# Moving the split weights' tiles by 64 bytes within the on-chip memory, in a two-block transformer kernel

## The chip, the cores and the metric

The kernel runs on one core of a Trainium2 chip. The metric is the device time of one execution, in microseconds (us). Before the change it is 1656.22 us, the median of three runs (1655.35 to 1659.63). Lower is better.

## The reference

Two small networks follow each other, all in float32, on 256 positions of width 1024. The first block has two layers. In each, a conditioning vector is multiplied with `w_ada` and gives shifts, scales and gates; a normed and modulated input is multiplied with `w_in`; a pooling mixer and a differential attention over 512 keys follow, then `w_out`, and a squared-relu MLP of width 4096. The first layer does this for the positions `x` and for the context `ctx`, the second for `x` alone. The second block has one layer with block attention and gated linear attention and one with a gated recurrence, each with a convolutional feed-forward network of width 3072.

```python
for l in range(DEPTH):                       # first block
    h = modulate(rms_norm(x, g_mix[l]), sa, ca)
    u, q, k, v = split_heads(h @ w_in[l])
    ...
    x = x + ga * (mix @ w_out[l])
    x = x + gm * sq_relu_mlp(modulate(rms_norm(x, g_mlp[l]), sm, cm), w_mlp1[l], w_mlp2[l])
for l in range(DEPTH):                       # second block
    h = h + mix
    h = h + conv_ffn(rms_norm_2(h, ffn_norm_g[l]), ffn_w_up[l], ffn_conv_w[l], ffn_conv_b[l], ffn_w_down[l])
```

What matters here: nearly all of the work is products of a [1024 or more, n] weight matrix, read once from HBM, with 256 (or 2 x 256) positions.

## The kernel before, in words

**The split products.** TensorE takes operands of type float32r here, which keep fewer bits than float32. To stay exact enough, each operand is held as two parts: `hi`, its value cast to float32r, and `lo`, the cast of what is left. A product is three matmuls: hi x hi, hi x lo and lo x hi. `unit` (L582) makes the list of calls and `issue` (L591) issues them, all on L593. Each is a matmul of a stationary 128x128 piece of the weights (`whi` or `wlo`) and a moving 128x256 piece of the data (`hid`, `fhi`, `flo`, `h2hi`, `dhi` and so on). There are 11,232 of them in the program, each with its own weight load.

**The stream of weights.** `Stream` (L72 to L175) brings every weight matrix in pieces of 1 MB: a DMA on SP fills a tile `raw` (three buffers of 8192 bytes in each partition). Each piece is two units of 128x1024 numbers. For a unit ScalarE casts `raw` to `whi` (L111), and VectorE subtracts and writes `wlo` (L119); there are four buffers of 4096 bytes of each. A unit feeds 24 matmuls on L593: 16 with `whi` (hi and lo data), then 8 with `wlo`, in the order of four output tiles. The order of all work is written out in the program: `gemm` (L597) issues six or so matmuls, steps a late eviction, lets the stream make a step (`tick`) and goes on.

**The conditioning.** Columns of `w_ada` come as tiles `araw` of 4096 bytes; VectorE multiplies them with a scalar column of `cs` and adds up (L278, L280), or TensorE does it with `cs` stationary (L293, L840) or `cr`, the split of `cs` (L837).

**Where the tiles lie.** Four pools stand one behind the other in each partition of the on-chip memory: `wp` (`raw`, `whi`, `wlo`, `araw`), `sp` (all data tiles and scratch), `cp` (constants and the residual `X`) and `mp` (small tiles). Within a pool, tags lie in the order of their first use. In `sp` the four buffers of `hid` follow each other in steps of 8192 bytes, and the six buffers of the other operands (`hhi`, `h2hi`, `fhi`, `dhi` ... with their lo parts) in steps of 8320. A `hid` or `fhi` piece k begins 1024 k bytes into its buffer; the pieces of `dhi` and `dlo`, where they carry two columns more (258), begin 1032 k bytes into it.

The lines that the change touches are L29 (which tags are small), L183 to L195 (the pools and `scr`), L755 and L823 (`cs` and `cr`).

Of the kernel before, what the change touches and what calls it, by code (L numbers as in the profile page):

```python
# [8 lines left out]
F32 = mybir.dt.float32  # L9
F32R = mybir.dt.float32r  # L10
# [15 lines left out]


MARKS = None
SMALL = {"tiny", "tiny4", "gs", "ared", "asum", "acol", "ld", "m2", "z2", "edge", "rtok", "gng", "aq4"}  # L29


def shape_constants():
# [141 lines left out]
def body(tc, I, out, dbg=None, stop=None):  # L174
    from contextlib import ExitStack  # L175
    with ExitStack() as es:
        _body(es, tc, I, out, dbg, stop)


def _body(es, tc, I, out, dbg, stop):  # L180
    nc = tc.nc
    mm, act, dve, pool_e, pe = nc.tensor.matmul, nc.scalar, nc.vector, nc.gpsimd, nc.tensor

    wp = es.enter_context(tc.tile_pool(name="wp", bufs=2))
    sp = es.enter_context(tc.tile_pool(name="sp", bufs=2))
    cp = es.enter_context(tc.tile_pool(name="cp", bufs=1))
    mp = es.enter_context(tc.tile_pool(name="mp", bufs=2))
    ps = es.enter_context(tc.tile_pool(name="ps", bufs=8, space=PSUM))
    st = Stream(nc, wp)

    def bank(shape=(128, 2, T)):
        return ps.tile(list(shape), F32, tag="ps", bufs=8, name="ps")

    def scr(shape, tag="s", bufs=5, dt=F32):
        return (mp if tag in SMALL else sp).tile(list(shape), dt, tag=tag, bufs=bufs, name=tag)  # L195

    def scr1(shape=(128, T)):
        return scr(shape, tag="s1", bufs=6)
# [17 lines left out]
    def mark(name):  # L216
        if MARKS is not None:
            MARKS.append((name, nc.next_id()))
# [47 lines left out]
    def ada_part(l, j, nv, ch, q):  # L266
# [20 lines left out]
        def rows(raw):  # L287

            if q == 0:
                acc[1] = bank([128, 512])  # L290
            p = acc[1]
            for k in range(2):
                mm(p[:2], cs[:, :, 2 * q + k], raw[:, k], start=q == 0 and k == 0, stop=q == 3 and k == 1)  # L293
            if q == 3:
                r = sp.tile([2, 512], F32, tag="aacc", bufs=1, name="arow")
                act.copy(r, p[:2])
                yield False
                c0 = 8 * j + 4 * ch
                p = bank([128, 8])
                for i in range(4):  # L300
                    pe.transpose(p[:, 2 * i:2 * i + 2], r[:, 128 * i:128 * i + 128], ident[:2, :2])
                yield False
                dve.tensor_add(ada[l][:, :nv, c0:c0 + 4], p[:, :8].rearrange("p (i v) -> p v i", v=2)[:, :nv],
                               pcol("b_ada", 48 * l + c0, 4)[:, None].to_broadcast([128, nv, 4]))
                if ch == 1:
                    done.add((l, j))
            yield True
# [3 lines left out]
    def ada_reduce(l, j, nv, ch, a):  # L311
        red = scr([128, 2, 16], tag="ared", bufs=1)
        for v in range(nv):
            dve.transpose(a[:, v], a[:, v])
            dve.reduce_sum(red[:, v], a[:, v].rearrange("p (b q) -> p b q", q=32), axis=AX)
        q4 = scr([32, 3, 2, 16], tag="aq4", bufs=1)
        for g in range(3):
            pool_e.tensor_copy(q4[:, g, :nv], red[32 * g + 32:32 * g + 64, :nv])
        s = scr([32, 2, 16], tag="asum", bufs=1)
        pool_e.tensor_add(q4[:, 0, :nv], q4[:, 0, :nv], red[0:32, :nv])  # L320
        pool_e.tensor_add(q4[:, 2, :nv], q4[:, 2, :nv], q4[:, 1, :nv])
        pool_e.tensor_add(s[:, :nv], q4[:, 0, :nv], q4[:, 2, :nv])
        col = scr([128, 2, 4], tag="acol", bufs=1)
        for g in range(4):
            pool_e.tensor_copy(col[32 * g:32 * g + 32, :nv],
                               s[:, :nv].rearrange("p v (j g) -> p v g j", g=4)[:, :, g])
        c0 = 8 * j + 4 * ch
        for v in range(nv):
            pool_e.tensor_add(ada[l][:, v, c0:c0 + 4], col[:, v], pcol("b_ada", 48 * l + c0, 4))
        if ch == 1:  # L330
            done.add((l, j))
# [90 lines left out]
    def transpose_params(b):  # L422
        p = bank([128, 128])
        pe.transpose(p[:, :nrow[b]], prow[b][:nrow[b], :], ident[:nrow[b], :nrow[b]])
        pb, c0 = place[b]
        dve.tensor_copy(pv[:, pb, c0:c0 + nrow[b]], p[:, :nrow[b]])
# [325 lines left out]


    ada = {l: mp.tile([128, 2, 48], F32, bufs=1, name=f"ada{l}") for l in range(2)}
    cs = mp.tile([128, 2, 8], F32, bufs=1, name="cs")  # L755
    mark("start")

    def load_ada0(k):
# [61 lines left out]
        dve.reciprocal(e, e)  # L820
        dve.tensor_mul(cs[:, v], e, pcol(name, 0, 8))

    cr = mp.tile([128, 8, 4], F32R, bufs=1, name="cr")  # L823
    act.copy(cr[:, :, 0:2], cs.rearrange("p v k -> p k v"))
    dve.tensor_sub(cr[:, :, 2:4], cs.rearrange("p v k -> p k v"), cr[:, :, 0:2])
    side = [first(0), first(1)]
# [650 lines left out]
    rtok = [rt[:, 1, tt:tt + 1] for tt in range(2)]  # L1477
# [85 lines left out]
    gng = scr([128, 4], tag="gng", bufs=1)  # L1563
# [485 lines left out]
```

## Time and profile before

| | |
|---|---|
| Median of 3 runs | 1656.22 us |
| The profiled execution: its own time | 1653.65 us |
| The profiled execution: span from first to last instruction | 1651.9 us |
| Mean granted TensorE clock, as a share of full speed | 0.97 |
| Busy: PE, PEld, DVE, ACT, POOL | 1571.6, 1475.2, 1221.6, 862.8, 82.5 us |
| HBM read | 253.83 MB |

The profile is of one execution. PE is TensorE's matmuls and PEld its weight loads, which run beside them; DVE is VectorE, ACT ScalarE, POOL GpSimd and SP the engine that issues most DMAs. Matmuls overlap each other in the trace, and each is shown with some 280 ns, so a matmul's own duration says little: the time that one costs in a dense stretch is the distance from its start to the start of the next. That is read from the time line, which gives the start of groups of equal instructions to 0.01 us: the distance between two starts divided by the matmuls that began in between.

### The profile page before, as it was taken

How to read it: one execution, taken by the hardware profiler on the slowest of the kernel's cores; microseconds unless marked ns; L12 is line 12 of the kernel's file. 1: busy time of each engine (PE TensorE's matmuls, PEld its weight loads, DVE VectorE, ACT ScalarE, POOL GpSimd, SP SyncE). 2: the span in 40 equal slices, each digit the busy share in tenths (PEclk: the TensorE clock that was granted, in tenths of full speed). 3: DMA queues.
4: the chain of work that ended last, by engine and by line, in shares of the span. 5: the costliest groups of instructions: out<-in, count | busy, mean ns of one | idle time of the engine just before them, and what ended most of it. 6: DMA issues, size and time to landing. Idle time of an engine off the chain costs nothing.

```text
span 1651.9 us, 31245 instructions
## 1 busy us (share of the span) xinstructions
PE 1571.6 (95%) x12917; PEld 1475.2 (89%) x12917; DVE 1221.6 (74%) x2105; ACT 862.8 (52%) x1471; POOL 82.5 (5%) x202
## 2 busy tenths in 40 slices
PE   7899798999999999798999999989999999899998
PEld 2886488999999999777999998669999998899998
DVE  6885478899978777656856677568886788897673
ACT  5646356522222225765744457436664558766463
POOL 0010000112121120000000000000000000000000
PEclk9999999999999999998999999779999999999999
DMA  9353323355455553212656554115655544555551
GB/s 367 121 153 106 122 90 118 128 179 180 155 202 192 192 180 109 77 52 90 211 179 202 179 179 129 52 58 175 203 180 180 198 153 159 179 178 185 178 197 55
DMA packets 134014, 256.89 MB, mean 156 GB/s; under 512 B 6224, under 2 KB 19184, under 8 KB 132848
## 3 DMA queue, kind: packets, MB, share of 16 engines
q1 hardware_dynamic: 132672, 254.31, 46.4%
q8 instruction: 101, 1.65, 0.4%
q10 hardware_dynamic: 1200, 0.59, 0.1%
q14 instruction: 41, 0.34, 0.1%
HBM read 253.83 MB, written 1.05 MB: 154 GB/s over the span
## 4 chain that ended last, share of the span: by engine, by line
PE 81%; DVE 8%; ACT 8%; issue 2%; DMA 1%; SPq 0%; DVEq 0%; ACTq 0%
PE ps L593 73%; DVE wlo L119 2%; ACT whi L111 1%; PE ps L987 1%; ACT s L922 1%; ACT s L524 1%; PE ps L293 1%; PE ps L1033 1%; ACT s L1002 1%; DMA raw<-in_w_ada_dram 1%; DVE s L942 1%; PE ps L1610 1%; DVE X L714 0%; PE ps L1024 0%; PE ps L1684 0%
## 5 line engine op out<-in xcount | busy, mean ns | idle before, releaser
L111 ACT CAST whi<-raw 128x1024 fp32r<-128x1024 f32 x380 | 394.2, 1048 | 427.5 <-PE ps L593 392.1
L119 DVE TENSOR_TENSOR wlo<-raw,whi 128x1024 fp32r<-128x1024 f32 x380 | 459.1, 1221 | 160.9 <-ACT whi L111 155.9
L593 PE MATMUL ps<-hid,whi 128*128 128x256 f32 x2304 | 295.5, 283 | 0.0
L593 PEld LDWEIGHTS ps<-hid,whi 128*128 128x128 f32 x2304 | 284.8, 192 | 0.0
L593 PE MATMUL ps<-h2hi,whi 128*128 128x256 f32 x672 | 162.2, 283 | 4.9 <-ACT h2hi L525 4.9
L593 PE MATMUL ps<-h2lo,whi 128*128 128x256 f32 x672 | 161.9, 281 | 0.0
L593 PE MATMUL ps<-hid,wlo 128*128 128x256 f32 x1152 | 156.8, 283 | 0.0
L593 PE MATMUL ps<-fhi,whi 128*128 128x256 f32 x640 | 155.3, 281 | 0.0
L593 PE MATMUL ps<-flo,whi 128*128 128x256 f32 x640 | 155.3, 281 | 0.0
L280 DVE SCALAR_TENSOR_TENSOR aacc<-araw,cs,aacc 128x512 f32<-128x512 f32 x182 | 129.1, 747 | 25.5 <-DMA araw<-in_w_ada_dram 24.6
L593 PEld LDWEIGHTS ps<-hid,wlo 128*128 128x128 f32 x1152 | 146.4, 192 | 0.0
L593 PEld LDWEIGHTS ps<-h2hi,whi 128*128 128x128 f32 x672 | 128.1, 191 | 5.3 <-ACT h2hi L525 5.3
L593 PEld LDWEIGHTS ps<-h2lo,whi 128*128 128x128 f32 x672 | 127.5, 190 | 0.3 <-DVE h2lo L527 0.3
L593 PE MATMUL ps<-dhi,whi 128*128 128x256 f32 (+1 forms) x512 | 126.5, 285 | 0.0
L593 PE MATMUL ps<-dlo,whi 128*128 128x256 f32 (+1 forms) x512 | 124.9, 281 | 0.0
L593 PEld LDWEIGHTS ps<-fhi,whi 128*128 128x128 f32 x640 | 121.1, 189 | 0.0
L593 PEld LDWEIGHTS ps<-flo,whi 128*128 128x128 f32 x640 | 120.5, 188 | 0.0
L593 PEld LDWEIGHTS ps<-dhi,whi 128*128 128x128 f32 x512 | 96.9, 189 | 0.5 <-issue 0.3
L593 PEld LDWEIGHTS ps<-dlo,whi 128*128 128x128 f32 x512 | 97.0, 189 | 0.2
L714 DVE SCALAR_TENSOR_TENSOR X<-ps,ada,X 128x256 f32<-128x256 f32 x184 | 75.9, 476 | 20.1 <-PE ps L593 20.1
L593 PE MATMUL ps<-fhi,wlo 128*128 128x256 f32 x640 | 89.3, 282 | 0.0
L593 PE MATMUL ps<-h2hi,wlo 128*128 128x256 f32 x672 | 88.8, 281 | 0.0
(392 smaller groups left out, 2820.4 us busy)
## 6 DMA issues: line engine op xcount, KB each, us to landing
raw<-in_w_mlp_dram SPq DMA_DIRECT2D x64, 1024.0 KB, 5.5
raw<-in_ffn_w_up_dram SPq DMA_DIRECT2D x48, 1024.0 KB, 5.1
araw<-in_w_ada_dram SPq DMA_DIRECT2D x80, 512.0 KB, 4.0
raw<-in_ffn_w_down_dram SPq DMA_DIRECT2D x24, 1024.0 KB, 5.3
raw<-in_w_in_dram SPq DMA_DIRECT2D x16, 1024.0 KB, 5.6
raw<-in_ev_w_in_dram SPq DMA_DIRECT2D x12, 1024.0 KB, 5.0
raw<-in_w_out_dram SPq DMA_DIRECT2D x8, 1024.0 KB, 4.8
raw<-in_od_w_in_dram SPq DMA_DIRECT2D x8, 1024.0 KB
```

The costliest lines, as they stand in the source:

```text
L111: self.nc.scalar.copy(hi, src)
L119: self.nc.vector.tensor_sub(lo, src, hi)
L280: dve.scalar_tensor_tensor(a[:, v], raw[:, k], c, a[:, v], op0=OP.mult, op1=OP.add)
L293: mm(p[:2], cs[:, :, 2 * q + k], raw[:, k], start=q == 0 and k == 0, stop=q == 3 and k == 1)
L524: act.activation(h, src, AF.Identity, bias=sa(n), scale=gs(n))
L593: mm(p, w, x, start=start, stop=stop, skip_group_check=True)
L714: dve.scalar_tensor_tensor(X[:, n, s], b[:, i], gates[s](n), X[:, n, s], op0=OP.mult, op1=OP.add)
L922: act.copy(sw[32 * q:32 * q + 32], src[32 * (q ^ 1):32 * (q ^ 1) + 32])
L942: dve.tensor_add(c[:, :, :width], a[:, :, :width], a[:, :, n:n + width])
L987: mm(sc[i][j][:, a], qT[64 * j:64 * j + 64, h, s * T + qt * 128:s * T + qt * 128 + 128], kT[64 * j:64 * j + 64, h, k0:k0 + nk], start=True ...
L1002: act.activation(ei[:, a], banks[j][:, a], AF.Exp, bias=m[:, j, a:a + 1], scale=0.125, accum_out=z[:, j, a:a + 1])
L1033: mm(p, v[:, kt, h * 128:(h + 1) * 128], t[:, i], start=i == 0, stop=i == len(keys) - 1)
```

## The change

Nothing is computed differently. Both programs have the same instructions in the same order on each engine, with the same waits; line numbers move by up to two. What differs is where tiles lie:

```diff
-SMALL = {"tiny", "tiny4", "gs", "ared", "asum", "acol", "ld", "m2", "z2", "edge", "rtok", "gng", "aq4"}
+SMALL = {"tiny4", "gs", "ared", "asum", "acol", "ld", "m2", "z2", "edge", "rtok", "gng", "aq4"}
...
     st = Stream(nc, wp)
 
+    cs = sp.tile([128, 2, 8], F32, tag="cs", bufs=1, name="cs")
+    cr = sp.tile([128, 8, 4], F32R, tag="cr", bufs=1, name="cr")
...
-        return (mp if tag in SMALL else sp).tile(list(shape), dt, tag=tag, bufs=bufs, name=tag)
+        return (mp if tag in SMALL else wp if tag == "tiny" else sp).tile(list(shape), dt, tag=tag, bufs=bufs, name=tag)
...
-    cs = mp.tile([128, 2, 8], F32, bufs=1, name="cs")
...
-    cr = mp.tile([128, 8, 4], F32R, bufs=1, name="cr")
```

The two `tiny` tiles (32 bytes each) move from `mp` into `wp`, where they come to lie between `raw` and `whi`; `cs` (64 bytes) and `cr` (128 bytes) move from `mp` to the start of `sp`. So `whi`, `wlo` and `araw` move up by 64 bytes, and all of `sp` and `cp` by 256. The addresses in each partition, from the two built programs:

```
tile                         before   mod 128  mod 256     after   mod 128  mod 256
raw, first buffer             16512      0       128       16512      0       128
whi, first buffer             41088      0       128       41152     64       192
wlo, first buffer             57472      0       128       57536     64       192
araw, first buffer            73856      0       128       73920     64       192
cs                           227616     32        32       82112     64       192
cr                           227744     32       160       82176      0         0
hid, first buffer             83072      0       128       83328      0       128
other operands, buffer 0     115840      0       128      116096      0       128
other operands, buffer 1     124160      0         0      124416      0         0
X                            210432      0         0      210688      0         0
```

The other buffers of `whi`, `wlo`, `araw` and `hid` have the same remainders as the first. Of the six buffers of the other operands, those with even numbers leave 128 after division by 256, and those with odd numbers 0. A 128x128 piece of the weights begins a multiple of 512 bytes into its half of the tile, so all pieces of the weights share the tile's remainder.

## Rows read from the trace of the kernel before

**Rows 1.** The page, part 1: busy time and share of each engine.
```profile
PE 1571.6 (95%) x12917; PEld 1475.2 (89%) x12917; DVE 1221.6 (74%) x2105; ACT 862.8 (52%) x1471; POOL 82.5 (5%) x202
```
**Rows 2.** The page, part 4: the chain that ended last, by engine and by line.
```profile
PE 81%; DVE 8%; ACT 8%; issue 2%; DMA 1%; SPq 0%; DVEq 0%; ACTq 0%
PE ps L593 73%; DVE wlo L119 2%; ACT whi L111 1%; PE ps L987 1%; ACT s L922 1%; ACT s L524 1%; PE ps L293 1%; PE ps L1033 1%; ACT s L1002 1%; DMA raw<-in_w_ada_dram 1%; DVE s L942 1%; PE ps L1610 1%; DVE X L714 0%; PE ps L1024 0%; PE ps L1684 0%
```
**Rows 3.** Windows of 100 us, all engines; (x) counts instructions that touch the window.
```profile
core 0: us, PE busy (x) PEld busy (x) DVE busy (x) ACT busy (x) POOL busy (x), PEclk, DMA share, GB/s
...
300.00:400.00 100.00, 100.00 (x846) 100.00 (x845) 93.23 (x146) 31.17 (x41) 17.55 (x36) 1.00 0.52 169
...
500.00:600.00 100.00, 100.00 (x845) 100.00 (x844) 77.04 (x118) 28.89 (x39) 21.27 (x55) 1.00 0.57 191
...
1200.00:1300.00 100.00, 100.00 (x842) 100.00 (x842) 73.02 (x108) 56.64 (x76) 0.00 (x0) 1.00 0.57 190
...
1500.00:1600.00 100.00, 100.00 (x841) 100.00 (x840) 72.82 (x107) 56.61 (x76) 0.00 (x0) 1.00 0.57 190
```
**Rows 4.** Time line of PE, hid with weights: start, length, what; ten units apart.
```profile
1292.49 2.08 PE L593 MATMUL ps<-hid,whi 128*128 128x256 f32 x16
1294.40 1.12 PE L593 MATMUL ps<-hid,wlo 128*128 128x256 f32 x8
...
1321.29 2.08 PE L593 MATMUL ps<-hid,whi 128*128 128x256 f32 x16
```
**Rows 5.** Time line of PE, first feed-forward network: fhi and flo, four units apart.
```profile
1165.99 1.11 PE L593 MATMUL ps<-fhi,wlo 128*128 128x256 f32 x8
...
1177.38 1.11 PE L593 MATMUL ps<-fhi,wlo 128*128 128x256 f32 x8
```
**Rows 6.** Time line of PE, last feed-forward network: fhi and flo, four units apart.
```profile
1508.84 1.12 PE L593 MATMUL ps<-fhi,wlo 128*128 128x256 f32 x8
...
1520.26 1.12 PE L593 MATMUL ps<-fhi,wlo 128*128 128x256 f32 x8
```
**Rows 7.** Time line of PE, MLP of the first layer: one double unit apart.
```profile
400.50 2.05 PE L593 MATMUL ps<-h2hi,wlo 128*128 128x256 f32 x16
...
406.14 2.05 PE L593 MATMUL ps<-h2hi,wlo 128*128 128x256 f32 x16
```
**Rows 8.** Groups by form: the matmuls with hid, and those where whi is moving.
```profile
L593 PE MATMUL ps<-hid,whi 128*128 128x256 f32 x2304 | 295.5, 283 | 0.0
L593 PE MATMUL ps<-hid,wlo 128*128 128x256 f32 x1152 | 156.8, 283 | 0.0
L593 PE MATMUL ps<-whi,hhi 128*128 128x256 f32 x128 | 31.8, 288 | 2.1 <-ACT whi L111 2.1
```
**Rows 9.** Time line of PE, MLP of the second layer: dhi and dlo with 258 columns.
```profile
793.81 1.13 PE L593 MATMUL ps<-dhi,wlo 128*128 128x258 f32 x8
...
805.34 1.14 PE L593 MATMUL ps<-dhi,wlo 128*128 128x258 f32 x8
```
**Rows 10.** Time line of PE, L1484: 24 matmuls with 16 stationary columns.
```profile
982.95 0.28 PE L1484 MATMUL ps<-dhi,prow 128*16 128x256 f32 x1
983.06 0.28 PE L1484 MATMUL ps<-dlo,prow 128*16 128x256 f32 x1
983.18 0.39 PE L1484 MATMUL ps<-dhi,prow 128*16 128x256 f32 x2
...
985.63 0.28 PE L1484 MATMUL ps<-dhi,prow 128*16 128x256 f32 x1
```
**Rows 11.** The page, part 5: the operations that write or read the moved tiles.
```profile
L111 ACT CAST whi<-raw 128x1024 fp32r<-128x1024 f32 x380 | 394.2, 1048 | 427.5 <-PE ps L593 392.1
L119 DVE TENSOR_TENSOR wlo<-raw,whi 128x1024 fp32r<-128x1024 f32 x380 | 459.1, 1221 | 160.9 <-ACT whi L111 155.9
...
L280 DVE SCALAR_TENSOR_TENSOR aacc<-araw,cs,aacc 128x512 f32<-128x512 f32 x182 | 129.1, 747 | 25.5 <-DMA araw<-in_w_ada_dram 24.6
```
**Rows 12.** One line, L517, which reads and writes at 1032 k bytes: duration minimum/median/maximum.
```profile
L517 DVE SCALAR_TENSOR_TENSOR dlo<-X,gs,dhi x24: 475/480/486, 255.3 to 791.4; 128x256 fp32r<-128x256 f32 x24
```
**Rows 13.** Waits of PE on L593 for the weights: us in total, times, longest.
```profile
PE ps L593 <- ACT whi L111: 8.9, 4, 3.3
PE ps L593 <- DVE wlo L119: 7.2, 5, 3.5
```

## The prediction, made before the changed kernel was run

> **What bounds the kernel now.** I read the page first, then windows, then the time line of PE. PE is busy for 95% of the span [rows 1], and the chain of waits runs over PE for 81%, over the split products of L593 alone for 73% [rows 2]. In the dense stretches PE has no idle time at all and the granted clock is 1.00, the higher of its two levels (2.4 GHz) [rows 3]. So the question is how fast matmuls follow each other there. A window of 40 us touches the 333 matmuls that start in it at 120 ns each and about two that began before; taking two off the counts of [rows 3], 839 to 844 matmuls start in 100 us: one in 118.5 to 119.2 ns. I take 119.0 ns as the mean of all dense stretches. Of the 11,232 matmuls on L593 some 11,000 run like that; the rest stand at waits. That is 11,000 x 0.119 = 1309 us, so **1 ns of this pace is worth 11 us**, and 0.3% of the time, which is about what a measurement of this kernel can tell from no change, is 5 us or 0.45 ns.
>
> The pace is not one number, and this is what the reader is to see. It differs by where the operands lie. I sort the stretches by the remainder of the moving operand's address by 256; that of the weights is 128 throughout, before the change.
> - Moving at 128 (every `hid` buffer): ten units of 24 matmuls in 1321.29 - 1292.49 = 28.80 us, 120.0 ns each [rows 4].
> - Moving at 0 (`fhi` and `flo` of the first feed-forward network, in buffers 3 and 5): four units in 11.39 us, 118.6 ns [rows 5].
> - Moving at 128 and 0 in turn (`fhi` in buffer 4, `flo` in buffer 5, of the last one): four units in 11.42 us, 119.0 ns [rows 6].
> - Moving at 0, 0, 128, 128 in turn (`h2hi` and `h2lo` of both segments in the first layer): 48 matmuls in 5.64 us, 117.5 ns [rows 7].
>
> Same columns, same clock, same engine: what sets these apart is how addresses stand to each other. The slowest pace belongs to the stretches where weights and data have the same remainder, and it is the steadiest too.
>
> **The change part by part.** No instruction, order or wait differs, so nothing is added or removed; only remainders change. The weights go from 128 to 192, and all moving operands keep theirs, since 256 bytes are added.
>
> *The stationary operand.* The relation of [rows 4], same remainder, no longer occurs anywhere. It held for 2304 + 1152 = 3456 matmuls with `hid` [rows 8] and for some 600 more whose buffers have the same remainder (counted from the addresses): 4,050. No row shows a stationary 128x128 piece 64 bytes off, so the cost has to be bounded. From below: with only 16 stationary columns, 23 distances take 985.63 - 982.95 = 2.68 us, 116.5 ns [rows 10]; a weight load that disturbs nothing leaves about this. From above: the `dhi` and `dlo` pieces with 258 columns are the ones that begin 8 to 56 bytes off a multiple of 128, and their four units take 11.53 us, 120.1 ns [rows 9], or 119.2 ns if taken down to 256 columns. The nearest rows are those whose relation is not the same-remainder one [rows 5 to 7], mean (118.6 + 119.0 + 117.5)/3 = 118.4 ns, since 64 bytes off is one more relation that is not the equal one. I take 118.4 for the 4,050, and leave the other 6,950 at what they have: (120.0 - 118.4) x 4,050 = **6.5 us less**.
>
> *The weights as moving operand.* In 384 matmuls of L593 (128 of them in [rows 8]) and 96 with 512 columns the weights move and now begin 64 bytes off. At the surplus of [rows 9] over 118.4 ns, 0.8 ns, that is 0.3 us more. In the other direction the row gives no gain.
>
> *The split itself.* ACT writes `whi` in 1048 ns and DVE `wlo` in 1221 ns for each unit [rows 11], beside 24 matmuls that take 2.86 us; PE waits for both together only 16.1 us in the whole span [rows 13]. An operation of DVE that reads and writes at remainders 0 to 56 keeps within 475 to 486 ns [rows 12], so I cost the 64 bytes at nothing. The cover is thin in one place: DVE is busy 93 of 100 us at 300 to 400 us [rows 3], where it also sums `araw` in pieces of 747 ns [rows 11]. If both grew by a tenth (some 35 x 0.12 + 60 x 0.075 = 8.7 us in that window) DVE would be late there, and PE would wait a few us for `wlo`.
>
> *DMA, `cs`, `cr`, `tiny`.* `raw` stays where it is. `araw` lands 64 bytes further, and a late one would show as the 24.6 us that DVE already waits for it [rows 11]; the small tiles are read a few dozen times. Nothing.
>
> The sum, against the profiled execution: 1653.65 - 6.5 + 0.3 = 1647.4 us. That execution ran 2.6 us under the median of the runs, 1656.22, so I forecast **1650.0 us**, 0.4% less. Its own range: were the 4,050 to go to 117.5 ns, 1646; were they to go to 119.0, 1652.
>
> One rule speaks against this. The Trainium skill, on the page "TensorE: Matmul & The Clock Gate", section "Step-by-step: what each phase is for", gives TensorE two independent read ports into SBUF, one for the streaming operand and one for the weight load. By that, where the weights lie against the data would not matter, and the change would give 1656. The trace disagrees in part: 117.5 to 120.0 ns by remainders alone.
>
> **The rivals.**
>
> *The weights' place is indifferent (no change).* The four paces could come from the moving operand alone: in all four relations the weights stand at 128, so the rows never vary them, and every difference between the rows could be one of data against data. For it: with 16 columns the distances are still uneven, 0.11 us and then 0.12 us at the start of [rows 10], so some of the unevenness is there without a full weight load. Then all stays at 1656.2.
> The Trainium skill, page "SBUF — State Buffer", section "Specifications (TRN2)", gives lines of 16 bytes with a penalty for each crossing into a new one. 64 is a multiple of 16, so by that rule no crossing is added, and the time would also stay; no row of mine shows a line's length.
>
> *Off the 128 costs (slower).* A piece of 512 bytes that begins 64 bytes past a multiple of 128 spans five such blocks and not four; if each block that is opened costs the load or the stream something, every matmul gets slower, not only those with `hid`. The place is the weight load beside each matmul of L593, and it decides as soon as the mean distance passes 119.0 ns. Price: at the unscaled pace of [rows 9], 120.1 ns, 1.1 x 11,000 = 12 us, 1668 us; if the same 1.1 ns comes on top of the 120.0 of `hid` for all, 121.1 ns, 23 us and 1679 us. For it: [rows 9] is the slowest stretch in the trace, and the only one off the 128. Against it: scaled to 256 columns it is 0.2 ns over the mean.
>
> *All relations get better (faster by much).* If a load 64 bytes off gets out of the stream's way everywhere, the pace falls to the 116.5 ns of [rows 10]: 2.5 x 11,000 = 27.5 us, 1629 us. ACT and DVE would keep up: 2.80 us for a unit against 1.05 and 1.22. Against it: nothing says why both remainders of the data should profit.
>
> **How the numbers follow.** My forecast has 0.38, of which 0.06 lies within 0.3% (a gain under 5 us); all relations better 0.14; indifferent 0.16; slower 0.32, of which 0.04 is too small to tell. So faster by over 0.3%: 0.32 + 0.14 = 0.46; within: 0.06 + 0.16 + 0.04 = 0.26; slower: 0.28. I put slower at almost a third because the change touches all 11,000 matmuls and the gain is argued for 4,050. The range reaches to 1622 on the fast side, a little past the pace of 16 columns, and to 1682 on the slow side, a little past 121.1 ns; beyond each I leave about 0.1.
>
> **What would show it.** Right: in the time line of PE the ten units with `hid` take about 28.4 us and no longer 28.80, at an uneven step, while four units with `fhi` still take 11.4. Indifferent: 28.80 and 11.39 again, to 0.02. Slower: the units of `fhi` and `h2hi` go to 2.88 us or more. In all cases the groups of L111 and L119 should keep their means of 1048 and 1221 ns, and PE's waits for them should stay near 16 us; if instead those means rise, the step "costed at nothing" is the wrong one. A pace under 116 or over 122 ns would make the whole bounding wrong.

## The result, and the profile after

| | before | after |
|---|---|---|
| Median | 1655.78 us (4 runs, 1653.62 to 1659.63) | 1632.01 us (4 runs, 1626.37 to 1637.41) |
| The profiled execution: its own time | 1653.65 us | 1626.37 us |
| Its span, mean granted clock | 1651.9 us, 0.97 | 1624.6 us, 0.973 |

The ratio is 0.9854, with a 95% interval from 0.9807 to 0.9900: the change makes the kernel about 24 us faster. A second series of the changed kernel (an experiment below) gave 1635.23 us, ratio 0.9876 (0.9859 to 0.9892), some 21 us.

The page of the changed kernel, part 1, answers to [rows 1]; the line of its chain of waits answers to [rows 2].

```profile
PE 1542.1 (95%) x12917; PEld 1448.1 (89%) x12917; DVE 1220.6 (75%) x2105; ACT 862.3 (53%) x1471; POOL 82.0 (5%) x202
...
PE 81%; DVE 8%; ACT 8%; issue 2%; DMA 1%; SPq 0%; DVEq 0%; ACTq 0%
...
L111 ACT CAST whi<-raw 128x1024 fp32r<-128x1024 f32 x380 | 393.9, 1047 | 404.0 <-PE ps L595 359.8
L119 DVE TENSOR_TENSOR wlo<-raw,whi 128x1024 fp32r<-128x1024 f32 x380 | 458.6, 1222 | 148.9 <-ACT whi L111 144.2
```

PE and PEld have become shorter, by 29.5 and 27.1 us; the other engines' busy time moved by 1 us or less. ACT and DVE write the moved tiles in 1047 and 1222 ns, as before [rows 11], and the bound is the same: PE 81% of the chain. The waits of PE for the weights, in the view of waits, stand where they stood [rows 13]:

```profile
PE ps L595 <- ACT whi L111: 9.1, 4, 3.3
PE ps L595 <- DVE wlo L119: 7.7, 5, 3.7
```

So the gain lies in the dense stretches. The windows of [rows 3], now, with PE idle in none of them (columns: window, length, then busy time and instructions touched of PE, PEld, DVE, ACT, POOL, granted clock, DMA share, GB/s):

```profile
300.00:400.00 100.00, 100.00 (x852) 100.00 (x852) 95.55 (x151) 29.84 (x39) 19.38 (x40) 1.00 0.55 180
500.00:600.00 100.00, 100.00 (x852) 100.00 (x851) 80.52 (x123) 30.25 (x41) 21.33 (x55) 1.00 0.57 193
1200.00:1300.00 100.00, 100.00 (x866) 100.00 (x865) 75.08 (x106) 55.74 (x74) 0.00 (x0) 1.00 0.58 190
1500.00:1600.00 100.00, 100.00 (x877) 100.00 (x876) 72.43 (x98) 55.51 (x72) 0.00 (x0) 1.00 0.54 180
```

At the same clock of 1.00 (2.4 GHz) 6 or 7 more matmuls fit into the first two windows, 24 and 36 more into the last two. The gain is uneven, and the time line of PE says how. First ten units with `hid` in the first feed-forward network, as in [rows 4] (start, length, what):

```profile
1278.71 1.98 PE L595 MATMUL ps<-hid,whi 128*128 128x256 f32 x16
...
1305.91 1.98 PE L595 MATMUL ps<-hid,whi 128*128 128x256 f32 x16
```

27.20 us for 240 matmuls, **113.3 ns** each, down from 120.0. The same `hid` buffers with the same relation of addresses, in the MLP of the first layer (48 matmuls from one row to the next), and in that of the second (seven units of 24 from the first row to the last):

```profile
331.01 3.93 PE L595 MATMUL ps<-hid,whi 128*128 128x256 f32 x32
336.66 3.93 PE L595 MATMUL ps<-hid,whi 128*128 128x256 f32 x32
...
825.71 2.05 PE L595 MATMUL ps<-hid,whi 128*128 128x256 f32 x16
...
845.50 2.05 PE L595 MATMUL ps<-hid,whi 128*128 128x256 f32 x16
```

5.65 / 48 and 19.79 / 168 are 117.7 and **117.8 ns**. So one relation has two paces. Now the first and the last feed-forward network, four units each as in [rows 5] and [rows 6], and `h2hi` of the first layer, one double unit as in [rows 7]:

```profile
1159.99 1.10 PE L595 MATMUL ps<-fhi,wlo 128*128 128x256 f32 x8
...
1171.30 1.10 PE L595 MATMUL ps<-fhi,wlo 128*128 128x256 f32 x8
...
1475.72 1.07 PE L595 MATMUL ps<-fhi,wlo 128*128 128x256 f32 x8
...
1486.82 1.07 PE L595 MATMUL ps<-fhi,wlo 128*128 128x256 f32 x8
...
402.57 2.05 PE L595 MATMUL ps<-h2hi,wlo 128*128 128x256 f32 x16
408.22 2.05 PE L595 MATMUL ps<-h2hi,wlo 128*128 128x256 f32 x16
```

11.31 / 96 = 117.8 (before 118.6), 11.10 / 96 = 115.6 (before 119.0), 5.65 / 48 = 117.7 (before 117.5).

Over all matmuls of the split products, counting as dense every distance from start to start of at most 135 ns, some 11,000 distances have a mean of 119.00 ns before and 116.82 after: 2.17 x 11,000 = 23.9 us less. By the data's place:

| data at (remainder by 256) | dense distances | before | after | us |
|---|---|---|---|---|
| 128 throughout | 3,760 | 119.99 | 115.99 | -15.0 |
| 0 throughout | 1,135 | 118.65 | 117.78 | -1.0 |
| mixed, and 8 to 56 off a multiple of 128 | 5,755 | | | -6.7 |
| weights moving | 356 | 118.79 | 115.40 | -1.2 |

### The profile page after: what moved, and what is told of

Its sections match the earlier page's. It is cut to its first block, busy times and chain, and to the rows that moved or that the text cites. A ratio compares the mean times of both kernels' runs of the same rounds, so it can differ in the third digit from the quotient of the medians.

```text
span 1624.6 us, 31245 instructions
## 1 busy us (share of the span) xinstructions
PE 1542.1 (95%) x12917; PEld 1448.1 (89%) x12917; DVE 1220.6 (75%) x2105; ACT 862.3 (53%) x1471; POOL 82.0 (5%) x202
## 4 chain that ended last, share of the span: by engine, by line
PE 81%; DVE 8%; ACT 8%; issue 2%; DMA 1%; SPq 0%; DVEq 0%; ACTq 0%
PE ps L595 74%; DVE wlo L119 2%; ACT whi L111 1%; ACT s L922 1%; ACT s L526 1%; ACT s L1002 1%; PE ps L987 1%; DVE s L942 1%; DMA raw<-in_w_ada_dram 1%; PE ps L295 1%; DMA araw<-in_w_ada_dram 1%; PE ps L1033 1%; DVE m L997 1%; PE ps L1610 0%; DVE wlo L448 0%
## 5 line engine op out<-in xcount | busy, mean ns | idle before, releaser
L111 ACT CAST whi<-raw 128x1024 fp32r<-128x1024 f32 x380 | 393.9, 1047 | 404.0 <-PE ps L595 359.8
L119 DVE TENSOR_TENSOR wlo<-raw,whi 128x1024 fp32r<-128x1024 f32 x380 | 458.6, 1222 | 148.9 <-ACT whi L111 144.2
L595 PE MATMUL ps<-hid,whi 128*128 128x256 f32 x2304 | 287.2, 280 | 0.0
L595 PEld LDWEIGHTS ps<-hid,whi 128*128 128x128 f32 x2304 | 276.7, 189 | 0.0
L595 PE MATMUL ps<-hid,wlo 128*128 128x256 f32 x1152 | 152.6, 279 | 0.0
L595 PEld LDWEIGHTS ps<-hid,wlo 128*128 128x128 f32 x1152 | 142.3, 189 | 0.0
L595 PEld LDWEIGHTS ps<-fhi,whi 128*128 128x128 f32 x640 | 120.1, 188 | 0.0
```

Of the source, the lines that this page charges most:

```text
L111: self.nc.scalar.copy(hi, src)
L119: self.nc.vector.tensor_sub(lo, src, hi)
L595: mm(p, w, x, start=start, stop=stop, skip_group_check=True)
```

## The experiments

All kernels here have the instructions, the order and the waits of the kernel before; only tiles lie elsewhere. What is compared is the **distance**: the remainder by 256 of (address of the weights' tile minus address of the data). Before the change it is 0 for data at 128 and 128 for data at 0; after it, 64 and 192. The theory that they test: the distance sets the pace, and nothing else does. The rivals: the weights' own place in a block of 128 bytes counts; or the data's; or the small tiles that were moved. The paces given without rows are means of a stage's dense distances in the trace. A time without a number of runs is of one execution; those of the kernel before lay between 1653.2 and 1659.6 us.

### The small tiles, and 256 bytes

The data moves up by 256 and `cs`, `cr`, `tiny` go where the change has them or near it, while the weights stay at 128.

```diff
+    cs = sp.tile([128, 2, 8], F32, tag="cs", bufs=1, name="cs")
+    cr = sp.tile([128, 8, 4], F32R, tag="cr", bufs=1, name="cr")
+    tinies = [sp.tile([128, 8], F32, tag=f"tiny{i}", bufs=1, name=f"tiny{i}") for i in range(2)]
```

> The weights' tiles stay at their old addresses (remainder 128 of 256); the data tiles lie 256 bytes further, and the small tiles cs, cr and tiny stand at the start of the data pool, as in the changed kernel but for tiny. If the 64 bytes of the weights made the gain: 120.0 ns per matmul with hid and 118.6 to 118.7 with fhi at remainder 0 again, and the time of the kernel before, 1650 to 1660 us. If the gain came from moving the small tiles or all data by 256 bytes: hid at 113 to 118 ns and a time near the changed kernel's, 1626 to 1637 us.

Measured: 1655.67 us, beside 1655.63 of the kernel before on the same chip; `hid` 120.00 ns, the first network 118.66. The small tiles and the 256 bytes do nothing. What the change does, it does by the weights' 64 bytes. That 256 bytes more between weights and data leave the pace as it was is also why the distance is taken by 256.

### Weights and data both 64 bytes further

`tiny` goes into `wp` as in the change, and `cs` and `cr` stay in `mp`: so weights and data all move by 64, and distances are as before.

> Weights and data both lie 64 bytes further (weights 192, hid 192, the other operands 192 and 64), so their distance is that of the kernel before. If the pace goes by the distance between the two addresses, it is 120.0 ns with hid and 118.7 with fhi in buffers 3 and 5, and the time 1650 to 1660 us. If it is the weights' own place in a block of 128 that counts, hid goes at 113 to 118 ns and the time is 1626 to 1640 us. If the start of the data in a block counts by itself, every stretch is slower, by the five blocks in place of four, over 120 ns.

Measured: 1656.30 us. The time line, nine units with `hid`:

```profile
1295.16 2.08 PE L593 MATMUL ps<-hid,whi 128*128 128x256 f32 x16
...
1321.08 2.08 PE L593 MATMUL ps<-hid,whi 128*128 128x256 f32 x16
```

25.92 / 216 = 120.0 ns, to the last digit [rows 4], though every piece of weights and data now begins 64 bytes past a multiple of 128. Nothing is lost or gained by lying off the 128: what counts is the distance.

### Weights at remainder 0, and at 64

`cr` (128 bytes) lies between `raw` and `whi` in the first of these; `cr` and the two `tiny` (192 bytes) in the second. The data stays where the change has it. The distances are 128 and 0, and then 192 and 64, for data at 128 and at 0.

```diff
+    cr = wp.tile([128, 8, 4], F32R, tag="cr", bufs=1, name="cr")
     apv = [bank([128, 512]) for _ in range(4)]
```

> Weights 128 bytes further (remainder 0), data as in the changed kernel (hid 128). By the distance: hid now stands as fhi at remainder 0 did before and goes at 118.6 to 118.7 ns, while fhi at remainder 0 stands as hid did and goes at 120.0; together 1645 to 1653 us. If only the remainder by 128 counts, all stays as before: hid 120.0, fhi 118.7, 1650 to 1660 us. If any move of the weights helped, hid would be at 113 to 118.

> Weights 192 bytes further (remainder 64), data as in the changed kernel. By the distance this is the changed kernel with the two kinds of data buffers exchanged: hid (128 - 64 = 64, as fhi at 0 against 192) at 117.8 ns throughout, and fhi at remainder 0 (0 - 64 = -64, as hid against 192) at 113.3 or 117.8 ns; 1630 to 1642 us. If only the remainder by 128 counts, it is the changed kernel again, hid at 113.3 in the last stages, 1626 to 1637 us. If the gain hung on 192 alone, 1650 us or more.

Measured: 1653.07 us with the weights at 0, at the very end of what was expected, and 1641.18 us at 64. Nine units with `hid`, and four with `fhi` of the first network, weights at 0:

```profile
1294.36 2.06 PE L596 MATMUL ps<-hid,whi 128*128 128x256 f32 x16
...
1319.99 2.06 PE L596 MATMUL ps<-hid,whi 128*128 128x256 f32 x16
...
1161.19 1.12 PE L596 MATMUL ps<-fhi,wlo 128*128 128x256 f32 x8
...
1172.71 1.12 PE L596 MATMUL ps<-fhi,wlo 128*128 128x256 f32 x8
```

25.63 / 216 = 118.7 ns for `hid`, 11.52 / 96 = 120.0 for `fhi`: the two paces of the kernel before have changed places, as their distances have. So the remainder by 128 alone does not do: by it, both would have stayed. With the weights at 64, `hid` (distance 192) has 117.78 ns in every stage; `fhi` of the first network (distance 64) 117.78 too, but `mlo` of the first layer, also at 64, has 113.33. Distance 64 shows two paces here as well.

### The distances between

With one small tile more or less ahead of `whi` and of the data, the weights go to 160 and 224.

```diff
+    gsub = wp.tile([128, 2], F32, tag="gsub", bufs=1, name="gsub")
+    nlam0 = sp.tile([128, 1], F32, tag="nlam0", bufs=1, name="nlam0")
```

> The weights' tiles lie 32 bytes past a multiple of 128 (remainder 160 of 256), the data where it was (remainders 128 and 0). So the distance weights minus data is 32 for data at 128 and 160 for data at 0, two distances not seen before. Theory (the pace depends on the distance alone, and falls off from its worst value at 0 as the distance grows): distance 32 somewhere between 113.3 and 120.0 ns, distance 160 between 117.8 and 118.7, so the mean between 116 and 119.3 ns and 1625 to 1659 us. Rival (only the 64-byte half of a line counts): distance 32 counts as 0 (120.0 ns) and 160 as 128 (118.65 ns), that is the times of the kernel before, 1656 us.

> The weights' tiles lie at remainder 224 of 256, the data at 128 and 0: distances 96 and 224. Theory (the pace depends on the distance alone and is best between 64 and 128 bytes ahead): distance 96 at or under 118.65 ns, distance 224 between 117.8 and 120.0; mean 115 to 118.5, 1614 to 1651 us. Rival (only the 64-byte half counts): 96 as 64 (113.3 or 117.8 ns) and 224 as 192 (117.8 ns), that is the paces of the changed kernel, 1626 to 1641 us.

Measured: 1652.04 and 1649.88 us, mean dense distances 118.29 and 118.09 ns. The theory's bands held for the times and the means, but not for two of the four distances: 160 has 120.0 ns, over its band, and 224 has 116.67, under its own; 96 passes its bound in one stage. So its form failed: the pace does not fall off smoothly from distance 0, for 160 costs as much as 0, and 224 is better than 96, where I had the reverse. The rival fell too: 32 does not count as 0, nor 96 as 64. With the kernels above, the paces in stretches where all matmuls have one distance are:

| distance | ns | where |
|---|---|---|
| 0 | 120.00 | `hid` before; `fhi` with weights at 0 |
| 32 | 118.33 | `hid`, weights at 160 |
| 64 | 113.33 or 117.78 | `hid` after; `fhi`, weights at 64 |
| 96 | 118.7, in one stage 120.00 | `hid`, weights at 224 |
| 128 | 118.66; in a short stage 120.00 | `fhi` before; `hid` and `dhi`, weights at 0 |
| 160 | 120.00 | `fhi`, weights at 160 |
| 192 | 117.78 | `fhi` after; `hid`, weights at 64 |
| 224 | 116.67; in a short stage 117.78 | `fhi` and `mlo`, weights at 224 |

The one stage at distance 96 that differs (the second product of the first network, eleven units) shows that the second pace is not a matter of distance 64 alone:

```profile
1291.04 2.08 PE L596 MATMUL ps<-hid,whi 128*128 128x256 f32 x16
...
1322.72 2.08 PE L596 MATMUL ps<-hid,whi 128*128 128x256 f32 x16
```

31.68 / 264 = 120.0 ns, where the other `hid` stages of that kernel have 118.5 to 118.7.

Where distances alternate, the pace is not the mean of theirs. In [rows 7] half of the matmuls stand at distance 0 and half at 128, and the pace is 117.5 ns, under the 120.0 and the 118.66 that these have alone. So the order in which distances follow each other counts too, and "nothing else does" holds only for stretches of one distance. Which order gives what pace was not tried.

### All data at distance 64, and at 0

The six buffers of the other operands, 8320 bytes each, leave 128 and 0 in turn. Given a tag each, with small tiles of 128 or 384 bytes in all between them, they all begin at 128, like `hid`.

```diff
+        if i in (1, 2):
+            ada[i - 1] = sp.tile([128, 2, 48], F32, tag=f"ada{i - 1}", bufs=1, name=f"ada{i - 1}")
...
-        return sp.tile([128, NT * (T + 2) + 16], dt, tag="h8", bufs=6, name=name)
+        t = sp.tile([128, NT * (T + 2) + 16], dt, tag=f"h8{H8[i]}", bufs=1, name=name)
```

`H8` lists the buffers in the order in which the kernel used them anyway.

> The changed kernel, with the six large buffers of the inputs placed so that all begin at remainder 128 of 256 like the four hidden buffers (small tiles lie between them); the weights stay at 192. So every dense matmul has the distance 64. Theory (the distance sets the pace): no dense matmul at the 118 ns of other distances by its own nature; each stage runs at one of the two paces that distance 64 has shown, 113.33 or 117.78 ns. All at 113.33 gives 1632 - 11,000 x 3.5 ns = 1594 us, all at 117.78 gives 1642 us; with the first block's stages at 117.78 as in the changed kernel and the rest at 113.33 about 1612 us; I expect 1600 to 1625. Rival (the gain hung on weights and data differing in their 64-byte half, and the mix of remainders 128 and 0 did not matter): as the changed kernel, 1626 to 1637 us.

> The kernel with all data at remainder 128, and the weights back at 128, where they lie before the change: the distance is 0 for every dense matmul, and nothing else differs from the kernel with distance 64 but the weights' 64 bytes. Theory (the distance sets the pace): every dense matmul at 120.0 ns, 1,656 + 11,000 x 1.0 ns = 1667 us, slower than the kernel before; no stage has a second value. Rival (it is the data buffers' being alike, or their new places, that gained): as the kernel with distance 64, 1600 to 1616 us.

Measured at distance 64: **1615.23 us** (4 runs, 1611.43 to 1615.66), ratio to the kernel before 0.9749 (0.9731 to 0.9766). Measured at distance 0: 1666.44 us, where 1667 was expected. Three units of the last feed-forward network, first at 64, then at 0:

```profile
1476.90 1.07 PE L614 MATMUL ps<-fhi,wlo 128*128 128x256 f32 x8
...
1485.06 1.07 PE L614 MATMUL ps<-fhi,wlo 128*128 128x256 f32 x8
```

```profile
1474.97 1.12 PE L616 MATMUL ps<-fhi,wlo 128*128 128x256 f32 x8
...
1483.61 1.12 PE L616 MATMUL ps<-fhi,wlo 128*128 128x256 f32 x8
```

8.16 / 72 = 113.3 ns against 8.64 / 72 = 120.0; at distance 0 every long dense stage of the program, the first network among them, has this pace. The two kernels differ in 64 bytes of the weights' place, and by 51 us. It is the distance, not the buffers' being alike.

### Which of the two paces

The changed kernel, and the one with all data at distance 64, once more.

> The changed kernel once more, to see whether its paces repeat. Its first trace has the hidden buffers' matmuls (distance 64) at 117.78 ns in both blocks of the first two layers' MLPs (322 to 598 us, 826 to 960 us) and at 113.33 ns in the last FFNs (from 1210 us). Theory A (the pace of a stage at distance 64 is a lock that is caught anew in each execution): some of these stages have the other value in this trace, and the times again spread over some 10 us. Theory B (the stage's own instructions fix it): every stage has the pace of the first trace within 0.3 ns, 1626 us, and the runs' spread comes from the clock alone.

> The kernel with all data at remainder 128 once more. Its first trace has 113.33 ns in the first MLP (324 to 620 us), 117.78 ns in the second (769 to 960 us), 113.33 ns from 1157 us. Theory A (caught anew): another set of stages at 117.78 ns, between 1594 and 1642 us; were the second MLP at 113.33 ns, its some 1,350 matmuls would give back 6 us, 1609 us. Theory B (fixed by the program): the same paces stage by stage, 1615 us.

> The kernel with distance 64 everywhere once more, for its times. Its two traces so far gave 1615 and 1603 us, the second with the second MLP at 113.33 in place of 117.78 ns and a higher granted clock in the mixer near 1050 us. Theory (each stage catches one of two paces anew): the executions fall between 1594 and 1620 us, and this trace has stages at 117.78 ns that are not all those of either trace before. Rival (the program fixes the paces and one of the two traces was an exception): all executions within 3 us of 1615 us.

Measured: the changed kernel 1635.23 us (4 runs, 1634.71 to 1636.03); the other 1602.55 us in the one run, then 1619.65 us (6 runs, 1607.24 to 1626.69), ratio 0.9768 (0.9734 to 0.9801). My 1594 to 1620 us was too low at its upper end: three of the six lie over it. The rival, all within 3 us of 1615, fell. Of the kernel with distance 64 everywhere there are now three traces. The MLP of the second layer, four units with `hid`, in the first and in the second of them:

```profile
822.07 2.05 PE L614 MATMUL ps<-hid,whi 128*128 128x256 f32 x16
...
833.38 2.05 PE L614 MATMUL ps<-hid,whi 128*128 128x256 f32 x16
```

```profile
821.80 1.98 PE L614 MATMUL ps<-hid,whi 128*128 128x256 f32 x16
...
832.68 1.98 PE L614 MATMUL ps<-hid,whi 128*128 128x256 f32 x16
```

11.31 / 96 = 117.8 ns and 10.88 / 96 = 113.3: one program, two executions, two paces. The third trace has 117.8 ns in the MLP of the first layer as well, where the others have 113.3 (48 matmuls; the third, then the first):

```profile
330.48 3.93 PE L614 MATMUL ps<-hid,whi 128*128 128x256 f32 x32
336.13 3.93 PE L614 MATMUL ps<-hid,whi 128*128 128x256 f32 x32
```

```profile
331.20 3.79 PE L614 MATMUL ps<-hid,whi 128*128 128x256 f32 x32
336.64 3.79 PE L614 MATMUL ps<-hid,whi 128*128 128x256 f32 x32
```

So here a stage catches one of two paces and keeps it, through hundreds of matmuls, until the stream breaks. The last product shows such a break: other matmuls (L2000) come in between twice, and behind them the same `hid` stage has the other pace. These rows are of the changed kernel; 48 matmuls lie between the first two and between the last two.

```profile
1596.74 1.07 PE L595 MATMUL ps<-hid,wlo 128*128 128x256 f32 x8
...
1602.18 1.07 PE L595 MATMUL ps<-hid,wlo 128*128 128x256 f32 x8
...
1603.77 1.05 PE L2000 MATMUL ps<-X 128*128 128x128 f32 x8
...
1605.37 1.05 PE L2000 MATMUL ps<-X 128*128 128x128 f32 x8
...
1606.73 1.10 PE L595 MATMUL ps<-hid,wlo 128*128 128x256 f32 x8
...
1612.39 1.10 PE L595 MATMUL ps<-hid,wlo 128*128 128x256 f32 x8
```

5.44 / 48 = 113.3 ns, then 5.66 / 48 = 117.9; the means of all five traces with `hid` at distance 64 go from 113.3 to 117.8 ns at this place.

In the kernel with distance 64 everywhere, the mean dense distance was 114.62, 113.97 and 115.74 ns in the three traces. The profiled executions of the second and the third took 1602.55 and 1622.90 us, and 1.77 ns x 11,000 = 19.5 us is nearly all of that. Over its eleven executions the median is 1615.33 us. In the changed kernel theory B came nearer: all long stages of the MLPs and the feed-forward networks repeated, to 0.02 ns, and only some shorter ones did not; its means are 116.82 and 116.81. What decides which pace is caught stays open: no kernel was run to force it.

So in the changed kernel the spread has, for the most part, another source. The two executions near 1627 us have a mean granted clock of 0.973, the six near 1636 us 0.961 to 0.968. The mixer of the second block, the same 634 matmuls: before, after, and after once more.

```profile
1067.70:1096.10 28.40, 23.69 (x634) 16.42 (x631) 13.51 (x36) 8.75 (x31) 0.00 (x0) 0.63 0.12 40
```

```profile
1060.10:1083.10 23.00, 18.98 (x634) 13.55 (x631) 12.51 (x33) 8.30 (x30) 0.00 (x0) 0.85 0.16 48
```

```profile
1062.60:1092.50 29.90, 24.63 (x634) 16.94 (x631) 13.99 (x36) 8.71 (x31) 0.00 (x0) 0.61 0.11 38
```

The profiled execution of the changed kernel was granted 0.85 there, between the levels of 1.2 and 2.4 GHz, and saved 5.4 us against before; the other one was granted 0.61 and lost 1.5. Of the 9.7 us between these two, 6.9 lie here. This is why the gain is 27 us between the two profiled executions and 21 to 24 by the medians, and 5 of the 27 have nothing to do with the dense pace. Whether the change has a part in that grant was not tested.

## Why the prediction was right, and where it was not

**What was right.** The bound (the distance from one matmul to the next in stretches without idle time), the worth of a nanosecond (11 us: 2.17 ns gave 24 us), and the reading that equal remainders are a bad relation, though not the only one (distance 160 has 120.0 ns too). The direction came true and the range, 1622 to 1682, held the result. The size did not come true: the gain is 24 us where some 6 were forecast. That the result lies in the range is luck in part: the forecast's own range ended at 1646, and the fast end of the stated one was set by the rival "All relations get better", which was given a chance of 0.14. ACT, DVE, DMA and the small tiles cost nothing, as costed: means of 1047 and 1222 ns, waits of 16.8 us in place of 16.1. The 24 matmuls with 16 stationary columns [rows 10] take 2.68 us again.

**The term that was mis-sized.** "I take 118.4 for the 4,050" made 6.5 us. The stretches of that relation went to 113.33 or 117.78 ns, 115.99 in the mean, and gave 15.0 us. The step took one more unequal relation to be like the unequal ones in the trace; in fact each distance has paces of its own, and 64 is the best of the eight tried. The 118.4 was not a price of unequal remainders either: by the addresses, two thirds of the matmuls in [rows 6] and half of those in [rows 7] have the equal remainder themselves, in turn with others. The lower bound, 116.5 ns from [rows 10], was none: some 1,500 matmuls run 3.2 ns under it. The prediction itself had named a pace under 116 as what would make its bounding wrong.

**The step that failed.** "Leave the other 6,950 at what they have." Their distance changed as well, from 128 to 192, and the mixed ones from 0 and 128 to 64 and 192; some 2,800 of the 6,950 had the equal remainder, counted from the addresses, but in streams where others had not. Together they made the time shorter by a further 7.7 us. The weights as moving operand, costed at 0.3 us longer, made it 1.2 us shorter, for as moving operand they change their distance too.

**The rivals.** "All relations get better" gave the time best, 1629 us, and for a half-right reason: most relations changed for the better here ([rows 7] and [rows 9] did not, 117.5 to 117.7 ns and 120.1 to 120.3), yet not since 64 bytes off is good in itself. With weights and data both 64 off, nothing moves. "Off the 128 costs" fell by the same kernel, 120.0 ns and 1656.30 us. "Indifferent" fell by the kernel with the weights at 0, where the data stands still and the paces of `hid` and `fhi` change places.

The trace of before could have warned of this: [rows 4] and [rows 5] give the pace at two distances, 0 and 128, and I read them as "equal" and "unequal". Two points do not say what a third distance does, and only the rival and the range allowed for that.

The kernel with the weights at 0 also weighs the rule that spoke against the change. By the Trainium skill, page "TensorE: Matmul & The Clock Gate", section "Step-by-step: what each phase is for", a weight load takes nothing from the streaming operand, as each has a read port of its own. The runs here disagree as to time, 113.3 to 120.0 ns by the distance of the two alone. The Trainium skill, page "SBUF — State Buffer", section "Specifications (TRN2)", has a penalty for each new line of 16 bytes. A cost of that kind, counted for each operand by itself, is the same for all the kernels above, whose tiles move by multiples of 32, and so does not give these differences.

## What to carry to other kernels

Where matmuls with a weight load each run back to back without idle time, read the distance of their starts from the time line and sort it by the addresses of weights and data together, not of either alone. Placing all data at one remainder and the weights 64 bytes further by 256 brought the time from 1656 to 1615 us (1602.55 to 1626.69 over eleven executions), with no operation added or taken away; it costs only an order of small tiles. Look at several executions before a verdict, since one program may run a stage at more than one pace.

## What was not expected of the hardware

- The pace of dense 128x256 float32r matmuls with a load each depends on the difference of the two operands' addresses by 256: eight distances gave 113.33 to 120.00 ns at a granted clock of 1.00, and moving both operands together changed nothing (120.00 again). Where distances alternate, the pace can lie under that of each (117.5 ns for 0 and 128 in turn). Why the difference sets the pace, no run here shows.
- It is not smooth in the distance: 118.33 ns at 32, 113.33 at 64, 118.66 at 128, 120.00 at 160, 117.78 at 192.
- A distance may have two paces, and a stage keeps the one it has caught: 113.33 or 117.78 ns at 64, in two executions of one program; 118.7 or 120.0 at 96. A break by other matmuls can change it, 113.3 to 117.9 ns within one product. At 0 only 120.0 was seen in long stages, in five kernels.
